# Modulation sums pinned to their traced place, decay vectors ahead of the first output projection, and low parts and other GpSimd work on VectorE between layers

## Chip, cores and metric

The kernel runs on one core of a Trainium2 chip. The metric is the device time of one execution in microseconds (us); the time before is 1883.51 us, the median of three runs (1880.94 to 1884.3).

## The reference, cut to what matters

Four layers run over 512 sample tokens and 128 prompt tokens of width 1024, with mixers in the order differential attention, retention, HGRN2, differential attention:

```python
for l in range(4):
    shift, scale, gate = split(silu(c) @ w_mod[l] + b_mod[l], 3)   # one set for samples, one for prompts
    h = rms_norm(x, g_pre[l]) * (1 + scale) + shift
    y = mixer[l % 3](h, w_in, w_out, ...)                          # ends in (o * silu(g)) @ w_out
    x = x + gate * rms_norm(y, g_post[l])
```

Retention also needs powers of a decay: `log_g = log1p(-exp(decay_param))`, sixteen numbers (two directions by eight heads), and from them the vectors that scale keys, queries and states.

## The kernel before, in words

All tokens stay on the chip as five tiles of 128 tokens (`NT`), four of samples and one of prompts. The products run on TensorE in three passes, since each operand is cut into a high part that ScalarE writes (`hi`) and a low part, the operand less its high part (`lo`, L116): `xh*wh + xh*wl + xl*wh`. Weights come by DMA as `raw`, are cut into `whi` (ScalarE, L178) and `wlo` (VectorE, L116), and at most four such pairs are live. The layer's input `h` is kept transposed as `hh` and `hl`.

**Order of the work.** The program is written with a scheduling layer. TensorE's instructions keep the order in which the program traces them. On every other engine the layer chooses the order ahead of time, by a model: where an engine is free it takes, of the instructions that are ready, the one traced first. So an instruction that is ready early can be put far ahead of its place in the trace. On the chip each engine then runs its queue strictly in that order. `tc.issue_after(ins)` makes what the block under it traces on `ins`'s engine stand behind `ins` in that queue.

**Modulation sums.** The vectors shift, scale and gate of a coming layer are summed while another layer runs. `w_mod` is loaded in pieces of four rows (`mraw`, two buffers, `mod_load` L324). `mod_next(rows)` (L351) adds `rows` to a debt, `mod_owed`, and as long as one row is owed and a piece is there it traces one row: two products of 128x256, on VectorE as `macc += raw * smod` (L371), or, for the first of a block's eight rows, on ScalarE (L369). In the attention layers every second row goes to ScalarE (L369) and is added on VectorE (L373). After eight rows a block is full; when row six of the next block is traced, `mod_turn` has TensorE transpose the full block (L339) and VectorE reduce it (L343). `weave` (L258) runs two generators into one another, the mixer's heads (main) and the projections for what comes next (fill); after each unit of fill it calls `mod_next(got * self.mod_pace)`, where `mod_pace` is four rows for each piece of the layer's list (`MOD_IN`: 24, 48, 0 and 8 pieces in the four layers) over `PACE` (155, 245, 195 by kind). `mod_finish` (L382), called when the fill reaches the tail of a layer, does all rows that are left and sets the debt to 0. The rest of that tail still calls `mod_next`.

**Between two layers** `out_layer` multiplies by `w_out`. Its last part runs, for each of the five tiles, 24 matmuls (`run`, the second half of the columns), then the norm: `square` on ScalarE, `norm` (VectorE L454 and L394, the power on GpSimd L401), `finish` (VectorE L553, times the gate), a copy of the first half from `yo` into `yg` on GpSimd (L614), `xt += yg * rs` on VectorE (L619), the DMA out (L620), `pre` (ScalarE L408, VectorE L394, GpSimd L401, ScalarE L410), which gives the next layer's normed tile `xh` (three buffers), and `turn` (L413): eight transposes on TensorE (L419), the modulation on VectorE (L421, L422), and `put_h`, the cut into `hh` (ScalarE L446) and `hl` (L116, on VectorE for tiles 0 and 4, on GpSimd for 1, 2 and 3). `step(tt)` are the 24 matmuls of the next layer's first projection for a tile. TensorE's order is run 0 to 3, turn 0, turn 1, run 4, turn 2, step 0, turn 3, step 1, turn 4, steps 2 to 4.

**Retention** (`ret` L875) begins with the decay vectors (L880 to L911: two DMAs, some twenty small instructions on VectorE and ScalarE, one of them the logarithm), then head 0's projections (`ret_proj`), and then, head by head, `weave(ret_mix(h), ret_proj(h + 1))`. `ret_proj` of a head gives 38.8 us of fill by its own count: 20 units of 1.3 for values and gates and 16 of 0.8 for queries and keys. It ends with the cut of the keys, `kh` on ScalarE (L922) and `kl` on VectorE (L116). `ret_mix` takes 3.5, 9 and 11 us of fill (`RW`) between its parts, the first right before it uses `kh` and `kl` (L929 to L931), and ends with `head_out` (VectorE L648). Each head also builds a table of decays: `tabt` on GpSimd (L958), then VectorE L959, ScalarE L960, VectorE L961.

Of the kernel before, what the change touches and what calls it, by code (L numbers as in the profile page):

```python
# [11 lines left out]
F32 = mybir.dt.float32  # L12
# [3 lines left out]
AF = mybir.ActivationFunctionType  # L16
ALU = mybir.AluOpType
# [4 lines left out]
P = 128  # L22
# [66 lines left out]
class Net:  # L89
# [260 lines left out]

    def mod_next(self, rows):  # L351

        nc = self.nc
        self.mod_owed += rows
        while self.mod_owed >= 1 and self.modr:
            self.mod_owed -= 1
            l, b, i, raw = self.modr[0]
            k = self.mod_row
            first = i == k == 0
            if first:  # L360
                self.macc = self.mp.tile([P, 2, 256], F32, tag="macc", bufs=2, name="macc")
            part = self.macc if first else None
            pool = self.mod_pool if k % 2 else None
            if pool is not None:
                part = pool.tile([P, 2, 256], F32, tag="mpart", bufs=2, name="mpart")
            for j in range(2):
                m, c = self.macc[:, j, :], self.smod[:, 4 * i + k, j:j + 1]
                if part is not None:
                    nc.scalar.activation(part[:, j, :], raw[:, k, :], AF.Copy, scale=c)  # L369
                else:  # L370
                    nc.vector.scalar_tensor_tensor(out=m, in0=raw[:, k, :], scalar=c, in1=m, op0=ALU.mult, op1=ALU.add)  # L371
            if pool is not None:
                nc.vector.tensor_tensor(out=self.macc, in0=self.macc, in1=part, op=ALU.add)  # L373
            if 4 * i + k == 5:
                self.mod_turn()
            self.mod_row = (k + 1) % 4
            if k == 3:
                self.modr.pop(0)
                if i == 1:
                    self.modp = (l, b, self.macc)  # L380
                self.mod_load()
# [30 lines left out]
    def turn(self, pool, l, tt, xh):  # L412

        nc = self.nc
        mt = self.mods[l]
        v = 0 if tt < 4 else 1
        pt = self.two([P, KT, P])
        for k in range(KT):
            nc.tensor.transpose(pt[:, k, :], xh[:, k * 128:k * 128 + 128], self.ident)  # L419
        h = pool.tile([P, KT, P], F32, tag="h32", bufs=2, name="h32")  # L420
        nc.vector.tensor_tensor(out=h, in0=pt, in1=mt[:, 8:16, v:v + 1].to_broadcast([P, KT, P]), op=ALU.mult)  # L421
        nc.vector.tensor_tensor(out=h, in0=h, in1=mt[:, 0:8, v:v + 1].to_broadcast([P, KT, P]), op=ALU.add)  # L422
        self.put_h(h, tt, nc.vector if tt in (0, 4) else None)

    def enter(self, l):

# [90 lines left out]
    def out_layer(self, l, y):  # L517
        nc, tc = self.nc, self.tc
        last = l == self.depth - 1
# [4 lines left out]
        with tc.tile_pool(name=f"op{l}", bufs=1, reuse_waits="tile") as op:  # L524
            w1 = self.take(l, 512, 4, op, nc.vector) if two else None
            xt = []
# [5 lines left out]
            yo = op.tile([P, NT, 2 if two else 1, 512], F32, name="yo")  # L532
            xh = {}
# [17 lines left out]
            def finish(tt, c, src, out):  # L551

                nc.vector.tensor_tensor(out=out, in0=src, in1=gb[:, 0 if tt < 4 else 1, c * 512:c * 512 + 512], op=ALU.mult)  # L553
# [53 lines left out]
            for tt in range(NT):  # L607
                ps = self.one()
                run(ps, tt, w1)
                if two:  # L610
                    nc.vector.tensor_tensor(out=yo[:, tt, 1, :], in0=yo[:, tt, 1, :], in1=ps, op=ALU.add)
                    ps = yo[:, tt, 1, :]
                yg = xh[tt] = op.tile([P, D], F32, tag="xh", bufs=3, name="xh")
                nc.gpsimd.tensor_copy(yg[:, 0:512], yo[:, tt, 0, :])  # L614
                square(tt, 1, ps)
                rs = self.norm(op, ssq[:, tt, :])
                finish(tt, 1, ps, yg[:, 512:1024])
                for c in (slice(0, 512), slice(512, 1024)) if last and tt == 4 else (slice(0, 1024),):
                    nc.vector.scalar_tensor_tensor(out=xt[tt][:, c], in0=yg[:, c], scalar=rs, in1=xt[tt][:, c], op0=ALU.mult, op1=ALU.add)  # L619
                    (nc.scalar if c.start else nc.sync).dma_start(self.x_out[tt][:, c], xt[tt][:, c])  # L620
                if not last:
                    self.pre(op, xt[tt], xh[tt])
                    for i in {3: (0, 1), 4: (2,)}.get(tt, ()):
                        self.turn(op, l + 1, i, xh[i])
            if not last:
                for tt in range(NT):
                    step(tt)
                    if tt < 2:
                        self.turn(op, l + 1, tt + 3, xh[tt + 3])


    def gate(self, o, ps):
# [239 lines left out]
        nc.vector.scalar_tensor_tensor(out=pr[1], in0=pr[1], scalar=rc, in1=pr[0], op0=ALU.mult, op1=ALU.add)  # L872


    def ret(self, l, y):  # L875
        nc, tc, t = self.nc, self.tc, self.t
        with tc.tile_pool(name=f"re{l}", bufs=1, reuse_waits="tile") as mp:
            self.gain = None
            rx = self.const(mp, "rx")
            rdec = self.const(mp, "rdec").rearrange("p (a b) -> p a b", a=2)  # L880
            rkd = self.const(mp, "rkd")
            e = mp.tile([P, 16], F32, name="dec_e")
            nc.sync.dma_start(e, t["ret_decay"][0].rearrange("a b -> (a b)").partition_broadcast(P))
            u = mp.tile([P, 16], F32, name="dec_u")
            d = mp.tile([P, 16], F32, name="dec_d")
            z = mp.tile([P, 16], F32, name="dec_z")
            lg = mp.tile([P, 2, 8], F32, name="lg")
            lgf = lg.rearrange("p a b -> p (a b)")
            ts_ = nc.vector.tensor_scalar
            nc.scalar.activation(e, e, AF.Exp)  # L890
            ts_(out=u, in0=e, scalar1=-1.0, scalar2=1.0, op0=ALU.mult, op1=ALU.add)
            ts_(out=d, in0=u, scalar1=1.0, scalar2=None, op0=ALU.subtract)
            ts_(out=z, in0=d, scalar1=0.0, scalar2=None, op0=ALU.is_equal)
            nc.vector.tensor_tensor(out=d, in0=d, in1=z, op=ALU.subtract)
            nc.vector.reciprocal(d, d)
            nc.vector.tensor_tensor(out=d, in0=d, in1=e, op=ALU.mult)
            nc.vector.tensor_tensor(out=z, in0=z, in1=e, op=ALU.mult)
            nc.scalar.activation(lgf, u, AF.Ln)
            nc.vector.tensor_tensor(out=lgf, in0=lgf, in1=d, op=ALU.mult)
            nc.vector.tensor_tensor(out=lgf, in0=lgf, in1=z, op=ALU.add)  # L900
            ts_(out=lgf, in0=lgf, scalar1=-1.0, scalar2=None, op0=ALU.mult)
            kd = mp.tile([P, 8, 6], F32, name="kd")
            for c0, c1, dr in ((0, 2, 0), (2, 4, 1), (4, 5, 0), (5, 6, 1)):
                n = c1 - c0
                nc.vector.tensor_tensor(out=kd[:, :, c0:c1], in0=rkd[:, c0:c1].unsqueeze(1).to_broadcast([P, 8, n]),
                                        in1=lg[:, dr, :].unsqueeze(2).to_broadcast([P, 8, n]), op=ALU.mult)
            nc.scalar.activation(kd, kd, AF.Exp)
            nlgb = mp.tile([P, 8], F32, name="nlgb")
            ts_(out=nlgb, in0=lg[:, 1, :], scalar1=-1.0, scalar2=None, op0=ALU.mult)
            cd = mp.tile([P, 2, 8], F32, name="cd")  # L910
            nc.scalar.activation(cd, lg, AF.Exp, scale=256.0)  # L911
            st = types.SimpleNamespace(mp=mp, l=l, lg=lg, kd=kd, cd=cd, rx=rx, rdec=rdec, nlgb=nlgb, h={})
            for _ in self.ret_proj(st, 0):
                pass
            for h in range(HEADS):
                fill = self.ret_proj(st, h + 1) if h < 7 else self.tail(l, y, 2, st)
                self.weave(self.ret_mix(st, h, y), fill, 1.0, 1.0 if h < 7 else RW[3])
# [15 lines left out]
    def ret_proj(self, st, h):  # L933
        nc, t, mp, lg = self.nc, self.t, st.mp, st.lg
# [20 lines left out]

        tab = hd.tab = mp.tile([P, 384], F32, tag="tab", bufs=2, name="tab")
        tb = mp.tile([P, 384], F32, tag="dq", name="tabt")
        nc.gpsimd.tensor_scalar(out=tb, in0=st.rx, scalar1=st.nlgb[:, h:h + 1], scalar2=None, op0=ALU.mult)  # L958
        nc.vector.scalar_tensor_tensor(out=tab, in0=st.rx, scalar=lg[:, 0, h:h + 1], in1=tb, op0=ALU.mult, op1=ALU.min)  # L959
        nc.scalar.activation(tab, tab, AF.Exp)  # L960
        nc.vector.scalar_tensor_tensor(out=tab, in0=st.rx, scalar=0.0, in1=tab, op0=ALU.is_equal, op1=ALU.add)  # L961
# [415 lines left out]
    def layers(self, depth):  # L1377
        nc, tc, t = self.nc, self.tc, self.t
# [13 lines left out]
        for l in range(depth):  # L1392
# [14 lines left out]
            with tc.tile_pool(name=f"y{l}", bufs=1, reuse_waits="tile") as yp_:  # L1407
                y = yp_.tile([P, NT, D], F32, name="y")
                (self.diff, self.ret, self.hg)[kind](l, y)
                self.out_layer(l, y)  # L1410
            self.x_in = self.x_out

# [31 lines left out]
```

## Time and profile before

| | |
|---|---|
| median of 3 runs | 1883.51 us |
| the profiled execution's own time | 1883.0 us |
| its span, first to last instruction | 1881.2 us |
| mean granted TensorE clock | 0.992 of full speed |
| TensorE matmul busy | 1803.2 us (96%) |
| VectorE, ScalarE, GpSimd busy | 1307.0 (69%), 981.3 (52%), 301.3 us (16%) |

PE is TensorE, PEld its weight loads, DVE VectorE, ACT ScalarE, POOL GpSimd, SP the queue that issues most DMAs. A matmul's shown time overlaps the next one's, so a busy PE is not a PE at its peak; an idle PE is lost time all the same, since its order is fixed and it is the busiest engine. Layer 0 runs to about 430 us, layer 1 to 1030, layer 2 to 1450, layer 3 to the end.

### The profile page before, as it was taken

Reading aid. Unit: us, or ns where it says so; the run is one execution under the profiler, and the core shown is the slowest. Engines: PE = TensorE matmul, PEld = TensorE weight load, DVE = VectorE, ACT = ScalarE, POOL = GpSimd, SP = SyncE. Lnnn points to the kernel's source line nnn. Section 1 sums busy time; section 2 is a strip of 40 time slices with the busy share of each in tenths; the row PEclk is TensorE's granted clock in tenths of the full one; section 3 lists DMA queues with packets and bytes.
Section 4 is the critical chain, followed back from the end, with each engine's and each line's share of the span. In section 5 each row is a group of like instructions: output and inputs, shape, how many; then the busy total and the mean of one; then the engine's idle time right before and its main releaser. Section 6 shows DMA issues by size and latency. Waiting matters only on the chain.

```text
span 1881.2 us, 31937 instructions
## 1 busy us (share of the span) xinstructions
PE 1803.2 (96%) x12060; PEld 1648.3 (88%) x12060; DVE 1307.0 (69%) x2681; ACT 981.3 (52%) x2271; POOL 301.3 (16%) x249
## 2 busy tenths in 40 slices
PE   6999999999999999999999999999979999999998
PEld 4889999977888888889878899999968889999976
DVE  4768888847788898873335666676774766767654
ACT  3556666645544444443333366666664645655552
POOL 0000000003222223222101223332331300000001
PEclk9999999999999999999999999999989999999999
DMA  9645455414354445443323322222214463443322
GB/s 302 181 122 151 146 146 166 122 51 157 117 160 146 149 150 158 124 135 101 115 93 101 96 71 66 63 63 74 62 43 135 140 171 91 116 114 100 100 73 101
DMA packets 231536, 224.39 MB, mean 119 GB/s; under 512 B 11619, under 2 KB 201558, under 8 KB 231382
## 3 DMA queue, kind: packets, MB, share of 16 engines
q1 hardware_dynamic: 230912, 221.96, 39.4%
q8 instruction: 95, 1.56, 0.4%
q14 instruction: 59, 0.48, 0.1%
q10 hardware_dynamic: 470, 0.39, 0.1%
HBM read 174.59 MB, written 18.35 MB: 103 GB/s over the span
## 4 chain that ended last, share of the span: by engine, by line
PE 62%; DVE 17%; ACT 8%; DMA 5%; issue 4%; POOL 2%; SPq 1%; DVEq 0%; ACTq 0%; POOLq 0%
PE one L474 6%; PE one L476 6%; PE one L475 6%; PE one L250 5%; PE one L251 5%; PE one L252 5%; DVE macc L371 3%; PE one L830 3%; PE one L225 3%; PE one L226 3%; PE one L227 3%; DVE wlo L116 2%; PE two L792 2%; PE two L793 2%; ACT whi L178 1%
## 5 line engine op out<-in xcount | busy, mean ns | idle before, releaser
L250 PE MATMUL one<-hh,whi 128*128 128x320 f32 x1152 | 364.6, 316 | 3.3 <-ACT qp L769 1.8
L252 PE MATMUL one<-hh,wlo 128*128 128x320 f32 x1152 | 356.1, 309 | 0.1
L251 PE MATMUL one<-hl,whi 128*128 128x320 f32 x1152 | 356.2, 309 | 0.0
L116 DVE TENSOR_TENSOR wlo<-raw,whi 128x1024 fp32r<-128x1024 f32 x192 | 235.8, 1234 | 142.6 <-ACT whi L178 142.1
L474 PE MATMUL one<-whi,hh 128*128 128x512 f32 x744 | 301.1, 405 | 6.5 <-ACT yo L569 3.2
L476 PE MATMUL one<-whi,hl 128*128 128x512 f32 x744 | 293.6, 395 | 1.7 <-DVE ms L394 1.3
L475 PE MATMUL one<-wlo,hh 128*128 128x512 f32 x744 | 292.2, 393 | 0.0
L178 ACT ACTIVATE whi<-raw 128x1024 fp32r<-128x1024 f32 x192 | 201.5, 1056 | 155.3 <-PE one L251 58.4
L250 PEld LDWEIGHTS one<-hh,whi 128*128 128x128 f32 x1152 | 216.9, 188 | 5.3 <-ACT qp L769 2.2
L251 PEld LDWEIGHTS one<-hl,whi 128*128 128x128 f32 x1152 | 217.1, 188 | 0.5
L252 PEld LDWEIGHTS one<-hh,wlo 128*128 128x128 f32 x1152 | 216.9, 188 | 0.4 <-DVE wlo L116 0.4
L401 POOL TENSOR_TENSOR rs<-ms,mhalf 128x1 f32<-128x1 f32 (+1 forms) x72 | 65.6, 913 | 901.3 <-DVE ms L399 724.8
L371 DVE SCALAR_TENSOR_TENSOR macc<-mraw,smod,macc 128x256 f32<-128x256 f32 x432 | 209.1, 527 | 0.2
L225 PE MATMUL one<-whi,hh 128*128 128x256 f32 x720 | 207.5, 288 | 0.0
L226 PE MATMUL one<-wlo,hh 128*128 128x256 f32 x720 | 200.8, 279 | 0.0
L227 PE MATMUL one<-whi,hl 128*128 128x256 f32 x720 | 200.8, 279 | 0.0
L474 PEld LDWEIGHTS one<-whi,hh 128*128 128x128 f32 x744 | 140.9, 189 | 36.9 <-DVE p L1017 4.0
L476 PEld LDWEIGHTS one<-whi,hl 128*128 128x128 f32 x744 | 140.5, 189 | 36.0 <-DVE hl L116 2.2
L475 PEld LDWEIGHTS one<-wlo,hh 128*128 128x128 f32 x744 | 140.9, 189 | 27.4
L225 PEld LDWEIGHTS one<-whi,hh 128*128 128x128 f32 x720 | 135.3, 188 | 1.5
L226 PEld LDWEIGHTS one<-wlo,hh 128*128 128x128 f32 x720 | 135.4, 188 | 0.0
L227 PEld LDWEIGHTS one<-whi,hl 128*128 128x128 f32 x720 | 135.0, 187 | 0.0
(345 smaller groups left out, 3548.6 us busy)
## 6 DMA issues: line engine op xcount, KB each, us to landing
mraw<-in_w_mod SPq DMA_DIRECT2D x96, 512.0 KB, 4.4
raw<-in_da_w_in SPq DMA_DIRECT2D x56, 512.0 KB, 4.5
raw<-in_hg_w_in SPq DMA_DIRECT2D x36, 512.0 KB, 3.9
raw<-in_ret_w_in SPq DMA_DIRECT2D x64, 256.0 KB, 3.1
kk<-ks SPq DMA_DIRECT2D x64, 160.0 KB, 2.8
kz<-ks SPq DMA_DIRECT2D x64, 160.0 KB, 2.8
qq<-q SPq DMA_DIRECT2D x64, 128.0 KB, 3.0
raw<-in_da_w_out SPq DMA_DIRECT2D x16, 512.0 KB, 3.4
```

The costliest lines, as they stand in the source:

```text
L116: return (eng or self.nc.gpsimd).tensor_tensor(out=out, in0=full, in1=hi.bitcast(F32), op=ALU.subtract)
L178: self.nc.scalar.activation(hi, raw, AF.Copy)
L225: mm(out, xh, wh[:, k % 4, :], start=(first and k == ks[0]), stop=False)
L226: mm(out, xh, wl[:, k % 4, :], start=False, stop=False)
L227: mm(out, xl, wh[:, k % 4, :], start=False, stop=(last and k == ks[-1]))
L250: nc.tensor.matmul(ps, wh[:, k, :], self.hh[:, k, c], start=(k == 0), stop=False)
L251: nc.tensor.matmul(ps, wh[:, k, :], self.hl[:, k, c], start=False, stop=False)
L252: nc.tensor.matmul(ps, wl[:, k, :], self.hh[:, k, c], start=False, stop=(k == KT - 1))
L371: nc.vector.scalar_tensor_tensor(out=m, in0=raw[:, k, :], scalar=c, in1=m, op0=ALU.mult, op1=ALU.add)
L474: mm(ps, xh, wh, start=(first and k == ks[0]), stop=False)
L475: mm(ps, xh, wl, start=False, stop=False)
L476: mm(ps, xl, wh, start=False, stop=(last and k == ks[-1]))
```

## The change

Four edits, all in the diff below. The modulation sums of a call of `mod_next` are put behind the VectorE and ScalarE instructions traced last before that call. The decay vectors move, unchanged, out of `ret` into a function `decay` that is traced after layer 0's mixer and before its output projection, in a pool that lives for the whole program. Between layers all low parts are made on VectorE, the GpSimd copy goes, the update of `xt` is two instructions of 512 columns and reads `yo` itself, and each turn of a tile comes one step later: run 0 to 3, turn 0, run 4, turn 1, step 0, turn 2, step 1, turn 3, step 2, turn 4, steps 3 and 4. `tabt` moves from GpSimd to VectorE.

```diff
     def mod_next(self, rows):
+        with ExitStack() as order:
+            for ins in self.traced():
+                order.enter_context(self.tc.issue_after(ins))
+            self.mod_rows(rows)
+
+    def traced(self):
+        found = {}
+        for ins in reversed(self.nc.cur_bb.bb.instructions):
+            if ins.engine in (mybir.EngineType.DVE, mybir.EngineType.Activation):
+                found.setdefault(ins.engine, ins)
+                if len(found) == 2:
+                    break
+        return list(found.values())
+
+    def mod_rows(self, rows):
         nc = self.nc
         self.mod_owed += rows
         while self.mod_owed >= 1 and self.modr:
...
-        self.put_h(h, tt, nc.vector if tt in (0, 4) else None)
+        self.put_h(h, tt, nc.vector)
...
                 yg = xh[tt] = op.tile([P, D], F32, tag="xh", bufs=3, name="xh")
-                nc.gpsimd.tensor_copy(yg[:, 0:512], yo[:, tt, 0, :])
                 square(tt, 1, ps)
                 rs = self.norm(op, ssq[:, tt, :])
                 finish(tt, 1, ps, yg[:, 512:1024])
-                for c in (slice(0, 512), slice(512, 1024)) if last and tt == 4 else (slice(0, 1024),):
-                    nc.vector.scalar_tensor_tensor(out=xt[tt][:, c], in0=yg[:, c], scalar=rs, in1=xt[tt][:, c], op0=ALU.mult, op1=ALU.add)
-                    (nc.scalar if c.start else nc.sync).dma_start(self.x_out[tt][:, c], xt[tt][:, c])
+                split = last and tt == 4
+                for c, half in ((slice(0, 512), yo[:, tt, 0, :]), (slice(512, 1024), yg[:, 512:1024])):
+                    nc.vector.scalar_tensor_tensor(out=xt[tt][:, c], in0=half, scalar=rs, in1=xt[tt][:, c], op0=ALU.mult, op1=ALU.add)
...
+                if not split:
+                    nc.sync.dma_start(self.x_out[tt], xt[tt])
                 if not last:
                     self.pre(op, xt[tt], xh[tt])
-                    for i in {3: (0, 1), 4: (2,)}.get(tt, ()):
-                        self.turn(op, l + 1, i, xh[i])
+                    if tt > 2:
+                        self.turn(op, l + 1, tt - 3, xh[tt - 3])
             if not last:
                 for tt in range(NT):
                     step(tt)
-                    if tt < 2:
-                        self.turn(op, l + 1, tt + 3, xh[tt + 3])
+                    if tt < 3:
+                        self.turn(op, l + 1, tt + 2, xh[tt + 2])
...
+    def decay(self):
+        nc, t, cp = self.nc, self.t, self.cp
...
+        self.decays = lg, kd, cd, nlgb
...
-        nc.gpsimd.tensor_scalar(out=tb, in0=st.rx, scalar1=st.nlgb[:, h:h + 1], scalar2=None, op0=ALU.mult)
+        nc.vector.tensor_scalar(out=tb, in0=st.rx, scalar1=st.nlgb[:, h:h + 1], scalar2=None, op0=ALU.mult)
...
                 (self.diff, self.ret, self.hg)[kind](l, y)
+                if l == 0:
+                    self.decay()
                 self.out_layer(l, y)
```

## Rows read from the trace of the kernel before

**Rows 1.** The page's first part: busy us, share of the span, instructions.
```profile
PE 1803.2 (96%) x12060; PEld 1648.3 (88%) x12060; DVE 1307.0 (69%) x2681; ACT 981.3 (52%) x2271; POOL 301.3 (16%) x249
```

**Rows 2.** Windows: stretch, length, busy us (instructions) of PE, PEld, DVE, ACT, POOL; PEclk.
```profile
65.00:112.00 47.00, 41.84 (x262) 39.59 (x260) 37.41 (x96) 25.58 (x67) 0.00 (x0) 0.96 0.73 210
115.00:350.00 235.00, 234.31 (x1830) 231.22 (x1828) 197.07 (x474) 157.60 (x443) 7.01 (x6) 1.00 0.48 138
440.00:480.00 40.00, 35.55 (x168) 28.86 (x167) 34.45 (x53) 19.13 (x31) 14.28 (x13) 0.96 0.38 122
505.00:520.00 15.00, 13.20 (x68) 10.50 (x67) 12.38 (x25) 7.21 (x16) 6.88 (x6) 1.00 0.31 89
520.00:840.00 320.00, 314.58 (x1849) 281.70 (x1848) 274.38 (x612) 136.21 (x308) 87.55 (x64) 1.00 0.48 148
1030.00:1056.00 26.00, 23.05 (x114) 18.95 (x113) 19.81 (x21) 10.87 (x16) 12.10 (x7) 1.00 0.21 72
```

**Rows 3.** Timeline between layers 0 and 1: start, us, instruction [idle before <-releaser].
```profile
463.79 3.03 DVE L371 SCALAR_TENSOR_TENSOR macc<-mraw,smod,macc 128x256 f32<-128x256 f32 x2
...
469.85 2.06 DVE L371 SCALAR_TENSOR_TENSOR macc<-mraw,smod,macc 128x256 f32<-128x256 f32 x5
...
471.58 1.09 PE L419 MATMUL two<-c_ident,xh 128*128 128x128 f32 x8 [3.50 <-ACT xh L410]
```

**Rows 4.** Groups by line: xcount | busy us, mean ns | idle before.
```profile
L619 DVE SCALAR_TENSOR_TENSOR xt<-xh,rs,xt 128x1024 f32<-128x1024 f32 (+1 forms) x21 | 27.9, 1334 | 11.0 <-POOL rs L401 11.0
L422 DVE TENSOR_TENSOR h<-h,modT 128x1024 f32<-128x1024 f32 x15 | 22.8, 1528 | 0.1
L116 POOL TENSOR_TENSOR hl<-h,hh 128x1024 fp32r<-128x1024 f32 x9 | 22.7, 2528 | 12.5 <-ACT hh L446 12.5
L421 DVE TENSOR_TENSOR h<-two,modT 128x1024 f32<-128x1024 f32 x15 | 18.0, 1217 | 7.4 <-PE two L419 7.4
L446 ACT ACTIVATE hh<-h 128x1024 fp32r<-128x1024 f32 x15 | 15.8, 1054 | 25.3 <-DVE h L422 25.2
L958 POOL TENSOR_SCALAR tabt<-c_rx,nlgb 128x384 f32<-128x384 f32 x8 | 13.2, 1652 | 14.7 <-DVE qd L978 8.1 <-DVE nlgb L909 6.5
```

**Rows 5.** Timeline between layers 1 and 2, the update of a tile.
```profile
1034.95 3.42 DVE L619 SCALAR_TENSOR_TENSOR xt<-xh,rs,xt 128x1024 f32<-128x1024 f32 x1 [0.43 <-POOL rs L401]
```

**Rows 6.** Waits of PE from 60 to 115 us: us, times, longest.
```profile
PE two L792 <- DMA raw<-in_da_w_in: 2.2, 1, 2.2
PE one L250 <- ACT qp L769: 1.3, 1, 1.3
```

**Rows 7.** Windows of L371 alone, 455 to 511 us: DVE busy (instructions).
```profile
455.00:511.00 56.00, 16.46 (x28) 0.97 0.37 116
```

**Rows 8.** Timeline at the start of layer 1.
```profile
485.68 1.28 ACT L898 ACT_TABLE_LOAD   x1
...
505.05 0.39 PE L474 MATMUL one<-whi,hh 128*128 128x512 f32 x1
...
506.44 0.60 PE L339 MATMUL one<-c_ident,macc 128*128 128x128 f32 x4
...
510.00 0.61 ACT L922 ACTIVATE kh<-k 128x512 fp32r<-128x512 f32 x1
...
511.26 0.68 DVE L116 TENSOR_TENSOR kl<-k,kh 128x512 fp32r<-128x512 f32 x1
```

**Rows 9.** Windows of DVE from a head's last L648 to the next kl.
```profile
556.10:568.00 11.90, 11.90 (x27) 1.00 0.62 194
667.40:678.30 10.90, 10.90 (x24) 1.00 0.52 159
```

**Rows 10.** The same windows, L371 alone.
```profile
556.10:568.00 11.90, 6.78 (x15) 1.00 0.62 194
667.40:678.30 10.90, 5.96 (x12) 1.00 0.52 159
```

**Rows 11.** Waits of PE from 520 to 840 us.
```profile
PE one L931 <- DVE kl L116: 1.8, 3, 0.6
```

More of the change, by code (lines that the diff above doesn't have):

```diff
@@ L617, in out_layer @@
                 finish(tt, 1, ps, yg[:, 512:1024])
-                for c in (slice(0, 512), slice(512, 1024)) if last and tt == 4 else (slice(0, 1024),):
-                    nc.vector.scalar_tensor_tensor(out=xt[tt][:, c], in0=yg[:, c], scalar=rs, in1=xt[tt][:, c], op0=ALU.mult, op1=ALU.add)
-                    (nc.scalar if c.start else nc.sync).dma_start(self.x_out[tt][:, c], xt[tt][:, c])
+                split = last and tt == 4
+                for c, half in ((slice(0, 512), yo[:, tt, 0, :]), (slice(512, 1024), yg[:, 512:1024])):
+                    nc.vector.scalar_tensor_tensor(out=xt[tt][:, c], in0=half, scalar=rs, in1=xt[tt][:, c], op0=ALU.mult, op1=ALU.add)
+                    if split:
+                        (nc.scalar if c.start else nc.sync).dma_start(self.x_out[tt][:, c], xt[tt][:, c])
+                if not split:
+                    nc.sync.dma_start(self.x_out[tt], xt[tt])
                 if not last:
                     self.pre(op, xt[tt], xh[tt])
-                    for i in {3: (0, 1), 4: (2,)}.get(tt, ()):
-                        self.turn(op, l + 1, i, xh[i])
+                    if tt > 2:
+                        self.turn(op, l + 1, tt - 3, xh[tt - 3])
             if not last:
@@ L872, in combine @@
         nc.vector.scalar_tensor_tensor(out=pr[1], in0=pr[1], scalar=rc, in1=pr[0], op0=ALU.mult, op1=ALU.add)
+    def decay(self):
+        nc, t, cp = self.nc, self.t, self.cp
+        rkd = self.const(cp, "rkd")
+        e = cp.tile([P, 16], F32, name="dec_e")
+        nc.sync.dma_start(e, t["ret_decay"][0].rearrange("a b -> (a b)").partition_broadcast(P))
+        u = cp.tile([P, 16], F32, name="dec_u")
+        d = cp.tile([P, 16], F32, name="dec_d")
+        z = cp.tile([P, 16], F32, name="dec_z")
+        lg = cp.tile([P, 2, 8], F32, name="lg")
+        lgf = lg.rearrange("p a b -> p (a b)")
+        ts_ = nc.vector.tensor_scalar
+        nc.scalar.activation(e, e, AF.Exp)
+        ts_(out=u, in0=e, scalar1=-1.0, scalar2=1.0, op0=ALU.mult, op1=ALU.add)
+        ts_(out=d, in0=u, scalar1=1.0, scalar2=None, op0=ALU.subtract)
+        ts_(out=z, in0=d, scalar1=0.0, scalar2=None, op0=ALU.is_equal)
+        nc.vector.tensor_tensor(out=d, in0=d, in1=z, op=ALU.subtract)
+        nc.vector.reciprocal(d, d)
+        nc.vector.tensor_tensor(out=d, in0=d, in1=e, op=ALU.mult)
+        nc.vector.tensor_tensor(out=z, in0=z, in1=e, op=ALU.mult)
+        nc.scalar.activation(lgf, u, AF.Ln)
+        nc.vector.tensor_tensor(out=lgf, in0=lgf, in1=d, op=ALU.mult)
+        nc.vector.tensor_tensor(out=lgf, in0=lgf, in1=z, op=ALU.add)
+        ts_(out=lgf, in0=lgf, scalar1=-1.0, scalar2=None, op0=ALU.mult)
+        kd = cp.tile([P, 8, 6], F32, name="kd")
+        for c0, c1, dr in ((0, 2, 0), (2, 4, 1), (4, 5, 0), (5, 6, 1)):
+            n = c1 - c0
+            nc.vector.tensor_tensor(out=kd[:, :, c0:c1], in0=rkd[:, c0:c1].unsqueeze(1).to_broadcast([P, 8, n]),
+                                    in1=lg[:, dr, :].unsqueeze(2).to_broadcast([P, 8, n]), op=ALU.mult)
+        nc.scalar.activation(kd, kd, AF.Exp)
+        nlgb = cp.tile([P, 8], F32, name="nlgb")
+        ts_(out=nlgb, in0=lg[:, 1, :], scalar1=-1.0, scalar2=None, op0=ALU.mult)
+        cd = cp.tile([P, 2, 8], F32, name="cd")
+        nc.scalar.activation(cd, lg, AF.Exp, scale=256.0)
+        self.decays = lg, kd, cd, nlgb
     def ret(self, l, y):
@@ L880, in ret @@
             rdec = self.const(mp, "rdec").rearrange("p (a b) -> p a b", a=2)
[L881 to L911, printed above, removed]
+            lg, kd, cd, nlgb = self.decays
             st = types.SimpleNamespace(mp=mp, l=l, lg=lg, kd=kd, cd=cd, rx=rx, rdec=rdec, nlgb=nlgb, h={})
```

## The prediction

> **What bounds the kernel now.** I began with the page's busy shares: TensorE is busy 96% of the span, VectorE 69%, ScalarE 52%, GpSimd 16% [rows 1]. TensorE's order is fixed by the trace of the program, so the change can only win back, or add, TensorE idle time and stretches at its low clock. The windows say where these lie near the change: in layer 0's start TensorE is busy 41.84 of 47 us, between layers 0 and 1 35.55 of 40, at layer 1's start 13.20 of 15, between layers 1 and 2 23.05 of 26; in the rest of layer 0 and in retention's first heads it is near full while VectorE is at 197.07/235 = 84% and 274.38/320 = 86% [rows 2]. That is the frame: some 15 us of idle time at four places, and two long stretches where VectorE has only 14 to 16% to spare.
>
> The timeline then says who causes the idle. Between layers 0 and 1 TensorE waits 3.50 us for an `xh` (L410) whose chain stands behind sums L371: two took 3.03 us beside a GpSimd low part, five 2.06 without one, 0.41 each [rows 3]. Though traced later, 28 sums ran between 455 and 511 us, 16.46 us of VectorE [rows 7]: the scheduler had moved layer 1's sums up into layer 0's tail. So far that when TensorE came to the first transposes of the sums (L339) at 506.44 us, before head 0's `kl` had even run (511.26) [rows 8], the block was finished.
>
> **The change, part by part** (against the profiled execution's own 1883.0 us, 1881.2 of it span; the median of the runs is 0.5 higher).
>
> *a. Start of layer 0.* Idle 47 − 41.84 = 5.2 us; the named waits are 1.3 for `qp` and 2.2 for weights [rows 6]. Sums pinned behind the rope's VectorE work no longer stand ahead of it, and their loads of `mraw` come later than the weights'. Bounds 0 and −5.2. I take −3, nearer the two waits (3.5) than the whole.
>
> *b. Rest of layer 0.* VectorE has 235 − 197.07 = 38 us free [rows 2], and takes the sums that (a) moves out, at 0.41 each [rows 3]. Nearly covered; bounds 0 and +4 (the weights' low parts could come late a few times). I take +1.
>
> *c. Between layers 0 and 1.* Idle 40 − 35.55 = 4.45, and a clock of 0.96 costs 40 × 0.04 = 1.6: 6.05 in all [rows 2]. A turn's path is now L421 1.2, L422 1.2 to 1.5, `hh` 1.05 [rows 4], and a low part of about 1.2 on VectorE in place of 2.53 on GpSimd [rows 4] (estimate: the L421 row, the same shape with two operands): some 4.7 us. TensorE runs 24 matmuls between a turn's transposes and their use; at 35.55/168 = 0.21 us [rows 2] that is 5.1, and the next turn's eight transposes add 1.09 [rows 3]. It fits, by 0.4 to 1.5 us. Splitting the update of `xt` adds less than the 0.41 us that a whole sum of 256 columns takes [rows 3], once a tile, inside the norm's own slack; the GpSimd copy vanishes off the path. Bounds 0 and −6.1; I take −5.6, since sums and GpSimd, both named by the wait, are gone.
>
> *d. Start of layer 1, the bill for (c).* `mod_finish` clears the debt when layer 0's tail begins, but the rest of that tail still calls `mod_next`: five units of 0.66, four of 3.9, one of 1.2 and four of 1.3 make 25.3 us of fill, times 96/155 = 0.62: 15.7 rows. No piece is loaded then, so all 16 rows are traced in one burst at layer 1's first unit of fill, right behind head 0's `kh` and `kl`. After eight of them comes the turn. Before, TensorE met it 506.44 − 505.05 = 1.4 us behind the last key projection X [rows 8]. Now it must wait for `kl` and seven rows of sums (the eighth is ScalarE's): 14 × 0.41 [rows 3] = 5.7 us. When is `kl` done? At the earliest X + 1.9: `kh` 0.61, `kl` 0.68 [rows 8] and about 0.6 to read the projection. At the latest X + 6.9 as before (511.26 + 0.68 − 505.05); but there the sums held it up. I take X + 2.9, near the early end. Stall: 2.9 + 5.7 − 1.4 = 7.2. After an idle stretch the clock fell in [rows 2] (0.96), costing 1.6; I add that, and take off the 15 − 13.20 = 1.8 idle that stands here now [rows 2]. Together +7.0. Bounds: +4 (early `kl`, no clock loss) and +11 (late `kl`).
>
> *e. Retention's heads with sums, five of them.* From a head's last L648 to the next head's `kl` VectorE is already without a gap: 11.90 of 11.90 and 10.90 of 10.90 us [rows 9], of which 15 and 12 sums are 6.78 and 5.96 [rows 10]. TensorE waits for that `kl` three times, 1.8 us together, at most 0.6 [rows 11]. `weave` spends 3.5 + 9 + 11 = 23.5 of a head's 38.8 us of fill between the parts of the head, so 15 are left behind its end: 15 × 4 × 48/245 = 12 rows, about 20 sums on VectorE. So about six more than now must pass before `kl`: 6 × 0.42 = 2.5 us. `tabt` on VectorE adds about 0.4 (1.65 on GpSimd [rows 4]; estimate from a 256-column sum at 0.41). Lower: the sums now run earlier in the head and slack takes it, less the GpSimd collisions removed, −2 in all. Upper: five heads × 2.4 = +12. I take +6, halfway: the full windows speak for the bill, and each wait's slack (at most 0.6 late now) is not seen.
>
> *f. Between layers 1 and 2.* Idle 26 − 23.05 = 2.95 [rows 2]. No sums run here; it is GpSimd: an `xt` update took 3.42 us [rows 5] against a mean of 1.33 [rows 4], beside a low part. All four low parts and the copy leave. Bounds 0 and −2.9; I take −2.7.
>
> *g. Decay vectors.* Some twenty small instructions, two DMAs on SP's queue and two loads of ScalarE's function table, 1.28 us each [rows 8], go to where layer 0 has a gap. ScalarE is at 157.60 of 235 there [rows 2], so I take +0.4; bounds 0 and 2 × 1.28 = +2.6. The Trainium skill, "ScalarE: Activation LUTs", section "What ACT_TABLE_LOAD costs", says a switch of set costs 1.28 us of load and then some 1.38 of drain, 2.66 in all; this case's row agrees on the load, and no row here shows the drain. By that page the upper bound would be 5.3, and the time in rival 4 below about 1891.
>
> Sum: −3 + 1 − 5.6 + 7.0 + 6 − 2.7 + 0.4 = **+3.1, so 1886.1 us**, some 1886.
>
> **Rivals.**
>
> *1. Faster.* VectorE's slack takes the heads (e between −2 and 0), and the burst is short (d at +4): −3 + 1 − 5.6 + 4 − 1 − 2.7 + 0.4 = −6.9, 1876. For it: a head still has 14% of VectorE free [rows 2]; against: none of it lies ahead of `kl` [rows 9].
>
> *2. Slower: sums ahead of `kl`.* One mechanism: pinned sums that VectorE cannot finish before TensorE needs `kl`, in every head in full (e +12) and at head 0 with the late `kl` (d +11). −3 + 1 − 5.6 + 11 + 12 − 2.7 + 0.4 = +13, 1896. It decides where more sums stand between a head's last L648 and `kl` than the 12 to 15 of now [rows 10], for with no gap there each further one costs 0.41 straight. For it: the waits for `kl` exist [rows 11]. Against: they are short.
>
> *3. The pin does not bind.* It puts sums behind the last traced instruction of the queue only; if that one is itself moved up, sums follow it. Then d and e fall away, the sums stay in (c), and only GpSimd's part goes: about half of (c) and all of (f), −3 − 2.7 = −6, 1877. Against: the last traced instruction is mostly one that waits for TensorE, and cannot move far.
>
> *4. Table loads on the path* (g +2.6): 1888. Against: ScalarE's free third of layer 0.
>
> **How the numbers follow.** The measurement tells about 0.2%, 3.8 us, from no change: 1879.7 to 1887.3 counts as the same. The forecast, 1881 to 1891, has 0.46 (0.28 within the band, 0.18 above, for e is open upward); rival 1, 1870 to 1880, 0.28 (0.26 faster, 0.02 the same); rival 2, 1891 to 1900, 0.16; rival 3 0.08 (0.07 faster, 0.01 the same); rival 4 0.02, slower. So faster 0.33, same 0.31, slower 0.36. The range 1874 to 1896 leaves out the outer parts of rivals 1 and 2, some 0.18; since cases of both signs hold most of the chance, the forecast's own 1881 to 1891 stands beside it.
>
> **What would show it.** Right: no L371 between layers 0 and 1, and L419 there without waits for `xh`; at layer 1's start one wait of TensorE at L339 for `macc`, about 7 us, with a dip of the clock behind it; in the heads longer waits of L931 for `kl`, 1 to 2 us each; no wait for `qp` at layer 0's start; no GpSimd low part between layers 1 and 2, and idle there near zero; the table loads before layer 0's end. Wrong: L339's wait missing or under 3 us (d falls, about 1880); waits for `kl` still under 0.6 (e falls, about 1880); sums still ahead of `kh` at layer 1's start (rival 3); TensorE waiting for `hl` or `xh` between layers (c and f fall, up to +8); new waits for `wlo` in layer 0's middle (b).

## The result and the profile after

The changed kernel takes 1908.93 us (median of 4 runs, 1907.49 to 1912.37) beside 1883.24 for the kernel before on the same chip: ratio 1.0139, 95% interval 1.0127 to 1.0151, 25.7 us slower. The forecast was 1886, within 1874 to 1896: wrong. The profiled execution took 1912.37 us, with a span of 1910.6, so the traces of the two differ by 29.4 us.

The page's first part, as in [rows 1]:

```profile
PE 1814.7 (95%) x12060; PEld 1652.0 (86%) x12060; DVE 1320.7 (69%) x2717; ACT 976.3 (51%) x2271; POOL 244.9 (13%) x212
```

No engine has much more to do: VectorE gains 14 us in all [rows 1], and GpSimd loses 56. Of the 29.4 us, 17.9 are time in which TensorE stands still (1910.6 − 1814.7 = 95.9 after, 1881.2 − 1803.2 = 78.0 before). The other 11.5 are TensorE's busy time, at a mean granted clock of 0.985 in place of 0.992. The clock is not the main thing: the fastest of the four runs had 0.992 too, and took 1907.49 us. The question is where the standing still lies. Line numbers moved: L371 is now L387, L369 L385, L419 L435, L619 L635, L823 L842, L931 L956.

TensorE issues 12060 matmuls in both kernels, in nearly the same order, so the start of the same matmul can be compared in two traces. The table gives, for the number of a matmul, how much later it starts than in the kernel before (minus is earlier); differences between columns are the price of a stage. Later experiments are in it too. Each row is one profiled execution, and these lie up to 5.2 us below (lag8) and 4.5 above (no_pin) the median of their kernel. For the heads (3300 to 5250), five kernels with the same pin in layer 1 show 14.1 to 17.3 us, so a difference of 3 us between two rows is no reading there.

```text
matmul number         500    590   2950   3150   3300   5250   6050   6300   9300   9900  12050
at, in before (us)    103    118    451    497    526    866   1025   1076   1467   1565   1872
after                -4.9   -1.4  +11.1   +4.5  +15.4  +29.6  +31.1  +28.9  +30.6  +30.9  +29.5
no_pin               -1.1   -1.1   -1.2   -3.7   -2.5   -0.6   +2.5   +0.3   -0.3   +5.0   +3.8
pin_only             -6.0   -2.8  +10.1   +3.4  +13.2  +27.9  +27.9  +28.4  +28.8  +27.7  +27.5
pin_after_layer0     -2.5   -2.3   -1.9   -8.4   +2.1  +19.4  +22.4  +20.2  +20.6  +20.4  +19.2
no_burst             -5.9   -2.7   +9.5   +2.9   +2.4  +28.2  +29.9  +27.7  +28.2  +27.9  +26.2
layer0_dve_only      -5.9   -3.2   +7.6   +1.2  +12.0  +27.5  +29.5  +27.3  +28.0  +27.0  +25.9
layer0_act_only      -5.9   -2.3   +5.9   -0.8  +11.3  +25.4  +28.4  +26.2  +25.8  +25.6  +24.6
lag8                 -5.9   +4.7   +9.5   +6.2   +5.9  +10.9  +11.0   +8.9   +6.8   +6.0   +4.8
floor                -2.0   -1.3   -1.6   -8.2   -6.5   -5.4   -5.3   -7.5   -5.4   -0.2   -1.3
mixed                -1.6   -1.0   -0.8   -6.4   -4.4   -3.1   -1.6   -3.9   -4.9   -6.1   -7.3
turn_late            -4.9   -1.6  +18.4  +13.0  +23.5  +38.4  +41.3  +39.2  +38.4  +38.1  +41.0
```

Row "after" gives the change by stage: the rest of layer 0 costs 12.5 us (−1.4 to +11.1), between layers 0 and 1 the change wins 6.6 (+11.1 to +4.5), the start of layer 1 costs 10.9, the heads with sums 14.2, and between layers 1 and 2 it wins 2.2. Three losses, two gains.

**Layer 0.** The two longest waits of TensorE from 115 to 350 us (us in total, times, longest); before, the list had one wait of 0.5 us:

```profile
PE one L849 <- ACT at L842: 7.4, 6, 2.3
PE one L839 <- ACT at L841: 2.3, 3, 0.9
```

The timeline at the longest of them, ScalarE and TensorE:

```profile
338.96 0.89 ACT L385 ACTIVATE macc<-mraw,smod 128x256 f32<-128x256 f32 x2
339.76 0.89 ACT L385 ACTIVATE mpart<-mraw,smod 128x256 f32<-128x256 f32 x2
340.56 0.58 ACT L841 ACTIVATE at<-one 128x512 f32<-128x512 f32 x1
341.04 0.27 ACT L842 ACTIVATE at<-one 128x128 f32<-128x128 f32 x1
...
341.35 0.38 PE L849 MATMUL one<-v,at 128*128 128x128 f32 x1 [2.29 <-ACT at L842]
```

Four products of sums stand right ahead of `at`, the copy that TensorE needs next: 1.6 us of sums (338.96 to 340.56) inside a wait of 2.29. VectorE's adds wait in turn, each for the product it takes in (DVE's waits in the same stretch):

```profile
DVE macc L389 <- ACT mpart L385: 11.0, 4, 4.0
```

**Between the layers.** The windows that answer to [rows 2] (the columns are those of [rows 2]), at their new places: between layers 0 and 1, start of layer 1, heads, between layers 1 and 2:

```profile
455.00:482.00 27.00, 26.48 (x132) 21.65 (x131) 19.56 (x27) 12.01 (x17) 3.75 (x6) 1.00 0.34 116
511.00:530.00 19.00, 8.65 (x38) 7.22 (x38) 16.19 (x38) 5.27 (x12) 0.59 (x1) 0.64 0.37 111
541.00:896.00 355.00, 342.99 (x1953) 302.03 (x1952) 282.78 (x627) 143.12 (x324) 76.27 (x61) 0.99 0.44 135
1061.00:1084.00 23.00, 22.94 (x111) 18.55 (x110) 17.30 (x22) 9.35 (x12) 3.58 (x4) 1.00 0.23 81
```

The idle of 4.45 us between layers 0 and 1 is down to 0.52 of 27, the 2.95 between layers 1 and 2 to 0.06 of 23, both at full clock. The window of L387 alone from 460 to 516 us shows no sum at all, where [rows 7] has 28:

```profile
460.00:516.00 56.00, 0.00 (x0) 0.98 0.28 95
```

**Start of layer 1.** What was taken away there comes due here: TensorE is busy 8.65 of 19 us, at 0.64 of its full clock. VectorE's timeline, and TensorE's behind it:

```profile
510.82 1.18 DVE L984 SCALAR_TENSOR_TENSOR tab<-c_rx,lg,tabt 128x384 f32<-128x384 f32 x1
512.59 0.56 DVE L986 SCALAR_TENSOR_TENSOR tab<-c_rx,tab 128x384 f32<-128x384 f32 x1 [0.59 <-ACT tab L985]
514.34 1.23 DVE L116 TENSOR_TENSOR wlo<-raw,whi 128x1024 fp32r<-128x1024 f32 x1 [1.19 <-ACT whi L178]
515.48 0.69 DVE L116 TENSOR_TENSOR kl<-k,kh 128x512 fp32r<-128x512 f32 x1
516.08 5.63 DVE L387 SCALAR_TENSOR_TENSOR macc<-mraw,smod,macc 128x256 f32<-128x256 f32 x14
...
509.54 0.39 PE L490 MATMUL one<-whi,hh 128*128 128x512 f32 x1
...
510.71 0.40 PE L492 MATMUL one<-whi,hl 128*128 128x512 f32 x1
521.46 1.21 PE L339 MATMUL one<-c_ident,macc 128*128 128x128 f32 x4 [10.35 <-DVE macc L387]
```

Right behind `kl` come 14 sums in 5.63 us, and TensorE waits 10.35 us for them at L339: about half of that for what stands ahead of the sums, half for the sums.

**Heads.** TensorE's longest waits from 541 to 896 us answer to [rows 11]:

```profile
PE one L339 <- DVE macc L387: 5.0, 5, 1.7
PE one L250 <- DVE sg L655: 2.8, 2, 1.4
PE one L956 <- DVE kl L116: 1.4, 1, 1.4
PE one L1045 <- DVE p L1042: 1.3, 1, 1.3
```

The wait for `kl`, 1.8 us in [rows 11], has not grown. The waits at L339 for the sums themselves are new, and the two at L250 took 1.6 us before. In the same matmuls before, TensorE was idle for 5.4 us, and after for 12.0 (third line of the four windows above):

```profile
525.59:866.37 340.78, 335.36 (x1953) 299.20 (x1951) 278.35 (x618) 144.11 (x323) 92.54 (x67) 1.00 0.46 140
```

That is 6.6 of the 14.2 us. The other 7.6 are busy time; two falls of the clock (last section) explain about half of it, and the rest has no name in the profile.

The length of a head is read from one `kl` to the next. One head before (from the second to the third `kl` after head 0's), then the same head after: all engines, then the sums alone.

```profile
622.70:678.40 55.70, 54.21 (x319) 48.38 (x317) 50.71 (x115) 24.58 (x55) 14.27 (x11) 1.00 0.49 153
622.70:678.40 55.70, 27.34 (x54) 1.00 0.49 153
```

```profile
640.80:699.10 58.30, 56.27 (x326) 49.51 (x324) 48.76 (x114) 24.02 (x56) 13.28 (x10) 1.00 0.46 144
640.80:699.10 58.30, 25.88 (x53) 1.00 0.46 144
```

VectorE does the same work, 54 and 53 sums among it, and is busy 50.71 of 55.70 us before and 48.76 of 58.30 after. The head is 2.6 us longer though VectorE is less full. It is order, not volume; the runs without the pin, below, bear this out.

### The profile page after: what moved, and what is told of

Same layout as the page of the kernel before. It is cut to its first block, busy times and chain, and to the rows that moved or that the text cites. A ratio compares the mean times of both kernels' runs of the same rounds, so it can differ in the third digit from the quotient of the medians.

```text
span 1910.6 us, 31838 instructions
## 1 busy us (share of the span) xinstructions
PE 1814.7 (95%) x12060; PEld 1652.0 (86%) x12060; DVE 1320.7 (69%) x2717; ACT 976.3 (51%) x2271; POOL 244.9 (13%) x212
## 4 chain that ended last, share of the span: by engine, by line
PE 61%; DVE 15%; ACT 10%; DMA 7%; issue 3%; SPq 3%; POOL 1%; ACTq 0%; DVEq 0%; POOLq 0%
PE one L492 7%; PE one L490 7%; PE one L491 7%; PE one L250 5%; PE one L251 5%; PE one L252 5%; PE one L849 3%; PE one L225 3%; PE one L226 3%; PE one L227 3%; DVE macc L387 2%; DVE wlo L116 2%; DMA mraw<-in_w_mod 2%; SPq L763 2%; ACT whi L178 2%
## 5 line engine op out<-in xcount | busy, mean ns | idle before, releaser
L250 PE MATMUL one<-hh,whi 128*128 128x320 f32 x1152 | 363.7, 316 | 2.8 <-DVE sg L655 2.8
L250 PEld LDWEIGHTS one<-hh,whi 128*128 128x128 f32 x1152 | 217.2, 189 | 4.2 <-issue 3.2
L387 DVE SCALAR_TENSOR_TENSOR macc<-mraw,smod,macc 128x256 f32<-128x256 f32 x432 | 207.9, 527 | 8.0 <-DMA mraw<-in_w_mod 6.0
```

The source lines that it names most:

```text
L250: nc.tensor.matmul(ps, wh[:, k, :], self.hh[:, k, c], start=(k == 0), stop=False)
```

## The experiments

The theory: the pin causes all of the loss, in three separate places, and the rest of the change is neutral or a small gain. The rival: the work moved to VectorE (the table of decays, the low parts) costs part of it.

### The change without the pin

```diff
     def mod_next(self, rows):
-        with ExitStack() as order:
-            for ins in self.traced():
-                order.enter_context(self.tc.issue_after(ins))
-            self.mod_rows(rows)
+        self.mod_rows(rows)
```

> The change without its pin: sums may be moved up again, the other three edits stand. Theory (the pin causes all of the loss): layer 0's middle, layer 1's start and the heads come back to the times of before (-12, -12 and -13 us against the changed kernel), idle between layers 1 and 2 stays gone (-2.5 against before), and part of the idle between layers 0 and 1 returns because the sums are there again: 1877 to 1881 us. Rival (the table of decays and the low parts on VectorE carry part of the loss in the heads): 1886 us or more, with waits of TensorE in retention's heads longer than before's.

Measured: 1882.23 us beside 1884.1, ratio 0.9991 (0.9980 to 1.0002): the time of before. The table's row no_pin shows none of the three losses; of the two gains, 2.5 us between layers 0 and 1 (−1.2 to −3.7), where sums run again, and 2.2 between layers 1 and 2 remain. It loses 5.3 us at the start of layer 3 (matmul 9300 to 9900), and it comes out above the theory's 1877 to 1881. The rival falls: the heads with sums come out 1.9 us above before in all (−2.5 to −0.6), of a loss of 14.2.

### The pin alone on the kernel before

```diff
+    def mod_next(self, rows):
+        with ExitStack() as order:
+            for ins in self.traced():
+                order.enter_context(self.tc.issue_after(ins))
+            self.mod_rows(rows)
+
...
-    def mod_next(self, rows):
+    def mod_rows(self, rows):
```

> The kernel before with the pin alone. Theory: all of the loss (+36 us in layer 0's middle, layer 1's start and the heads) and some 4 us of gain between layers 0 and 1, where GpSimd's low parts stay; between layers 1 and 2 as before: 1911 to 1916 us. Rival (part of the loss is the table of decays on VectorE and the vectors' move): 1895 to 1905 us.

Measured: 1914.88 us, ratio 1.0175 (1.0152 to 1.0199), as the theory said, and the three losses stand at the same places (12.9, 9.8 and 14.7 us). Between layers 0 and 1 the pin alone wins 6.7 us, between layers 1 and 2 nothing. So the pin alone brings the whole first gain (the rest of the change, without it, 2.5), and the second belongs to the work taken off GpSimd.

### The pin from layer 1 on

```diff
+            self.pin = l > 0
...
-            for ins in self.traced():
+            for ins in self.traced() if self.pin else ():
```

> The change with the pin only from layer 1 on. Theory (in layer 0 the pinned products on ScalarE and adds on VectorE wait for one another and hold up the attention's copies): layer 0 is 11 us shorter, the rest as in the changed kernel: 1897 to 1899 us, no waits of TensorE for the copy `at` (L842, 7.4 us) between 115 and 350 us. Rival (the sums that are not done in layer 0's start must be done somewhere in layer 0, and cost the same wherever they stand): 1905 us or more.

Measured: 1902.99 us, ratio 1.0103 (1.0087 to 1.0119). Layer 0 is fully mended: −1.9 in place of +11.1 at 451 us, and between 115 and 350 us TensorE waits for one thing, shortly:

```profile
PE one L839 <- DVE pe L891: 0.6, 1, 0.6
```

The total is 4 us above the theory's range all the same, because the heads took more in this execution, 17.3 us in place of 14.2, though layer 1 is pinned just as in the changed kernel: that is scatter. The rival's claim, that the sums cost the same wherever they stand in layer 0, falls.

### One of the two queues pinned in layer 0

```diff
+            self.pin = l > 0
...
             for ins in self.traced():
-                order.enter_context(self.tc.issue_after(ins))
+                if self.pin or ins.engine == mybir.EngineType.DVE:
+                    order.enter_context(self.tc.issue_after(ins))
```

The second kernel has `Activation` in place of `DVE`.

> The change with only VectorE's instructions pinned while layer 0 runs (ScalarE's products free), both from layer 1 on. Theory (the 13 us of layer 0 need both pins: an add in its place on VectorE waits for a product that stands late on ScalarE, up to 4.0 us, and holds up what is behind it): layer 0 ends 2 to 6 us later than with no pin there: 1903 to 1908 us less the heads' scatter. Rival (VectorE's pin alone does it): layer 0 12 us or more later, as in the changed kernel.

> The change with only ScalarE's products pinned while layer 0 runs (VectorE's sums and adds free), both from layer 1 on. Theory (both are needed): layer 0 ends 2 to 6 us later than with no pin there. Rival (ScalarE's pinned products alone stand in front of the copies `at` that TensorE waits for): 10 us or more later, and the waits for L842 are back.

Measured: 1911.66 us (ratio 1.0151, 1.0133 to 1.0170) and 1911.83 (1.0150, 1.0124 to 1.0175), which the medians cannot tell from the full change. The table is finer: with no pin in layer 0 matmul 2950 is at −1.9, with VectorE's alone at +7.6, with ScalarE's alone at +5.9, with both at +11.1. Either costs 8 to 10 us, both together 13. So the theory that it takes both falls; so does each rival that one does all, though with ScalarE's alone the waits for `at` are back as that rival said. TensorE's waits from 115 to 350 us with ScalarE pinned alone (lines one higher than in the changed kernel):

```profile
PE one L850 <- ACT at L843: 6.6, 6, 2.6
```

and with VectorE pinned alone (the longest two):

```profile
PE one L850 <- ACT at L843: 3.6, 4, 1.1
PE one L840 <- ACT qp L789: 2.6, 1, 2.6
```

ScalarE's pinned products stand ahead of `at` directly. With VectorE pinned alone ScalarE is late too, for its products now wait for VectorE's pinned adds, 13.5 us in this stretch (3.2 with no pin in layer 0), and what is behind them in its queue waits along:

```profile
ACT mpart L386 <- DVE macc L390: 13.5, 15, 1.9
```

### No burst at the start of layer 1

```diff
+            self.mod_owed = 0
             self.mod_pace, self.mod_pool = ...
```

> The change with the debt cleared when a layer begins, so that the 16 rows of the burst are spread over the layer by the pace instead. Theory (the wait of 10.4 us at L339 is the burst's): the wait at the first L339 of layer 1 falls to under 2 us with the clock dip behind it gone, 1897 to 1900 us. Rival (rows left out of the burst are paid for later, at other turns or at the end of the layer, where the rest of the rows are finished): 1903 us or more.

Measured: 1906.26 us, ratio 1.0122 (1.0107 to 1.0137). The burst's wait is gone: the start of layer 1 costs −0.5 (+2.9 to +2.4) in place of 10.9. And the rival is right about the rest: the heads cost 25.8 us in place of 14.2, and more sums stand in them (319 of L387 from 529 to 894 us, 296 after). TensorE's longest waits in the heads, 529 to 894 us:

```profile
PE one L956 <- DVE kl L116: 5.1, 4, 2.1
PE one L1045 <- DVE modT L343: 3.7, 2, 1.8
PE one L339 <- DVE macc L387: 3.5, 4, 1.2
```

With a pinned order the rows cost about the same at once or spread (25.1 us for start and heads together after, 25.3 here), so the burst was not just one bad place.

### The transposes of a block two rows later

```diff
-            if 4 * i + k == 5:
+            if 4 * i + k == 7:
                 self.mod_turn()
```

> The change with the transposes of a full block (L339) traced two rows later, right behind row eight of the next block in place of row six. Theory (in the heads TensorE mostly waits at L339 for the last pinned sums of a block, 5.0 us and two dips of the clock): those waits shrink, heads of 57 us in place of 58.5, the burst's wait as before: 1901 to 1905 us. Rival (the order on VectorE holds up the head's own work, and TensorE waits for that instead): heads of 58 us or more, waits for `kl`, `p` and `sg` longer, 1906 us or more.

Measured: 1921.38 us, ratio 1.0184 (1.0165 to 1.0203), the slowest of all. In the heads the wait at L339 nearly goes, and `kl` takes its place (TensorE's longest waits, 560 to 900 us):

```profile
PE one L956 <- DVE kl L116: 5.0, 4, 2.2
PE one L490 <- DVE p L1042: 2.3, 2, 1.3
PE one L250 <- DVE sg L655: 2.3, 2, 1.4
PE one L1045 <- DVE p L1042: 1.8, 1, 1.8
PE one L339 <- DVE macc L387: 0.8, 1, 0.8
```

The rival holds: whichever of VectorE's results is asked for first is late. The 12 us more come mostly from layer 0, which this edit moves too: matmul 2950 is 7.3 us later than in the changed kernel, TensorE now waiting at L339 between 115 and 350 us (5.3 us for VectorE's `sg`, 2.2 for ScalarE's `hsq`). Layer 3 behind its start adds 4.4 (matmul 9900 to 12050).

### Pins that leave some freedom

Two kernels let a sum move up, but not without bound. In the first it may stand up to eight calls ahead of its place:

```diff
+        self.back = (self.back + [self.traced()])[-9:]
         with ExitStack() as order:
-            for ins in self.traced():
+            for ins in self.back[0]:
```

> The change with each call's sums pinned not behind the newest VectorE and ScalarE instructions but behind those that were newest eight calls earlier, some 8 to 10 us of fill. Theory (the heads lose because a sum may not use the holes just ahead of its place): heads of 55 to 56.5 us in place of 58.5, layer 0's middle near the time of before: 1885 to 1894 us. Rival (sums must be moved up far, by a head or more, to help): heads of 58 us again, 1902 us or more.

In the second a layer's sums are kept behind the layer's start and nothing else, and the debt is cleared:

```diff
+            self.mod_owed, self.floor = 0, self.traced() if l else []
...
-            for ins in self.traced():
+            for ins in self.floor:
```

> The change with the sums of a layer kept behind the start of that layer only (no other pin), and the debt cleared when a layer begins. Theory (moving up within a layer is what the heads need, moving up across the start of layer 1 is what hurts): layer 0 as without the pin, between layers 0 and 1 as in the changed kernel (no sums, no wait for `xh`), a wait at the first L339 of layer 1 under 2 us, heads of 55 to 56 us each: 1874 to 1879 us, the fastest of all. Rival (the 30 sums that ran between the layers are missing later, and the heads take them on at their full price): heads of 57 us or more, 1884 us or more.

Measured: eight calls of freedom give 1892.85 us, ratio 1.0044 (1.0024 to 1.0063), with the heads' loss down from 14.2 us to 5.0 (+5.9 to +10.9), in an execution 5.2 us below the median. The rest of layer 0 costs 4.9 (+4.7 to +9.5) in place of 12.5; but 10.6 us are lost earlier, between 103 and 118 us, where TensorE waits 9.0 us for the attention's `pe` and `at`. The total is the theory's case, at its upper end. The floor gives 1883.63, ratio 1.0006 (0.9995 to 1.0018). The same head as above, all engines and the sums alone:

```profile
615.20:670.40 55.20, 54.76 (x321) 48.67 (x320) 50.88 (x112) 24.07 (x55) 13.32 (x10) 1.00 0.51 155
615.20:670.40 55.20, 27.86 (x56) 1.00 0.51 155
```

56 sums in a head of 55.20 us: that a sum may move up inside its layer is worth nearly all of the heads' loss (−6.5 to −5.4 is 1.1 left), and keeping it out of the stretch between the layers wins 6.6 us (−1.6 to −8.2) with only 1.7 given back behind it. The total misses the theory's 1874 to 1879 by what is lost at the start of layer 3: −5.4 to −0.2 from matmul 9300 to 9900, as in the kernel without the pin.

### Each stage in its best order

```diff
+            self.mod_owed, self.layer = 0, l
+            self.floor = self.traced() if l else []
...
-            for ins in self.traced():
+            for ins in self.traced() if self.layer == 3 else self.floor:
```

> The change with each place given the order that its run was best in: no pin in layer 0, sums of layer 1 kept behind the layer's start (debt cleared), the pin as in the changed kernel in layer 3. Theory (the free sums of layer 3 stand ahead of its rope and cost the 5 to 6 us seen there): 1877 to 1880 us, faster than both. Rival (layer 3's 6 us are scatter of its start, or the pinned sums cost as much later in the layer, as in layer 0): 1882 to 1886 us.

Measured: 1875.68 us (1872.41 to 1877.05) beside 1885.02, ratio 0.9948 (0.9935 to 0.9961): 0.5% faster than before and, by the two ratios (0.9948/1.0139), 1.9% faster than the changed kernel, a little under the range that the theory gave. With layer 3 pinned its start loses nothing (−4.9 to −6.1), as in every kernel pinned there, so the rival falls. The theory's reason, free sums ahead of the rope, is not shown: the kernel before, unpinned, has the same 12 sums and 24 products in that stretch as floor and no_pin, and takes 98.0 us for it, where they take 103. That the pin costs nothing here goes with a low pace, 32 rows over the whole layer; in layer 0 it is three times that.

## Why the prediction was wrong, step by step

- **b, rest of layer 0: the step that failed most.** Predicted +1, bounds 0 to +4; measured +12.5. "Nearly covered" rested on a share: 38 us free of VectorE in 235. A pinned sum cannot use free time that lies ahead of the place to which the pin ties it; with eight calls of freedom this stretch costs 4.9. And ScalarE's products, half the rows in the attention layers, were given no cost at all; alone they cost 8 us.
- **e, heads: the wrong deadline.** Predicted +6, upper bound +12; measured +14.2. The step put the whole bill on `kl`, about six more sums ahead of it in every head and waits of 1 to 2 us. There were between one and two more: between a head's last L667 (L648 before) and the next `kl` stand 16, 16, 10, 16 and 18 sums, where 15, 14, 12, 13 and 14 stood. The first and the third head, which answer to [rows 10]:

```profile
570.00:583.30 13.30, 6.95 (x16) 1.00 0.57 169
685.60:699.10 13.50, 4.25 (x10) 1.00 0.56 168
```

TensorE waited for `kl` once, 1.4 us, less than the 1.8 before. It waited instead at L339 for the pinned sums themselves (5.0 us, none before), and longer at L250 (2.8 for `sg`, 1.6 before), and the clock fell behind two of the waits. The step took one deadline for the bill where every result of VectorE is one. In no_burst and turn_late `kl` did become the longest wait, 5.1 and 5.0 us.
- **d, the burst: the mechanism was right, the size at its upper bound.** Predicted +7.0 (up to +11), measured +10.9. The 14 sums took 5.63 us (5.7 predicted). The term that was mis-sized is `kl`. The prediction's X, the start of the first 512-column matmul behind the key projection (505.05 in [rows 8]), lies at 509.54 us here; TensorE reached L339 at 511.11, 1.6 behind it (1.4 predicted), but `kl` ended at 516.17, 6.6 behind it in place of 2.9. The prediction took 2.9 because sums were said to have held up the 6.9 of before. That reading was wrong: VectorE's timeline of before shows no sum from 500 us to `kl` at 511.26, only the work that stood ahead of `kl` again, the decay table and a weight's low part above all. ScalarE's `kh`, at 514.60, was late behind the same table and the same weight.
- **c and f, between the layers: right.** −5.6 predicted, −6.6 measured, half a us beyond the bound; −2.7 and −2.2. No sum was left in the stretch, no wait for `xh` in either. For (c) the prediction named sums and GpSimd; pin_only wins all of it with GpSimd's work still there.
- **a, start of layer 0:** −3 predicted, −1.4 measured. The gain reached 4.9 at 103 us, the waits for weights and `qp` were gone, and 3.5 of it was given back within 15 us, where TensorE waited 3.4 for the attention's `pe` instead and the clock fell (a mean of 0.91 from 98 to 116 us). What is left is not the pin's for certain: without it (no_pin) this stage is 1.1 shorter too.
- **g, decay vectors: right, nothing seen.** Both table loads moved to the start of the program, where ScalarE has idle time; TensorE's longest wait from 25 to 60 us is 1.9, for a result of VectorE, as before (1.8):

```profile
35.89 1.28 ACT L914 ACT_TABLE_LOAD   x1
37.19 0.22 ACT L914 ACTIVATE lg<-dec_u 128x16 f32<-128x16 f32 x1
...
41.65 1.28 ACT L927 ACT_TABLE_LOAD   x1
42.94 0.22 ACT L927 ACTIVATE cd<-lg 128x16 f32<-128x16 f32 x1
```

The next ScalarE instruction starts 1.30 and 1.29 us behind a load. The drain of 1.38 us that the Trainium skill, "ScalarE: Activation LUTs", section "What ACT_TABLE_LOAD costs", adds to a load does not show here; the rows decide, and a switch cost 1.3.

With the terms as measured (−1.4 + 12.5 − 6.6 + 10.9 + 14.2 − 2.2, and 2.1 us scattered over the rest) the sum is +29.5, as the traces differ. Rival 2, pinned sums that VectorE cannot finish in time, came nearest to the mechanism; it was priced at 1896 because it had only `kl` for a deadline, which was not the one missed in the heads, and nothing in layer 0. Rival 3, a pin that does not bind, is excluded by the empty window of L387; rival 4 by the table loads' place.

## What to carry to other kernels

That an engine is 15% free in the mean does not say that work with a fixed place in its queue is free: holes ahead of that place are lost to it, and results behind it can come later. Here this cost in layers 0 and 1, and nothing in layer 3, where a third as many rows as in layer 0 were pinned. Work with a distant due time should have a window, a bound that keeps it from moving too far up, not an exact place. When a pin is priced, count each engine that it ties and each result asked for behind it, not only the one that was late before.

## What was not expected of the hardware

That short waits can double in price. At the wait of 10.35 us at the start of layer 1 TensorE's clock fell to the lower of its two levels (1.2 GHz), and behind the one of 3.50 us in [rows 3] it had done so before; but in the heads it fell behind waits below 2 us too, at 749 and 811 us. It did not behind every such wait: four others of 1.3 to 1.4 us, for `sg`, `p` and `kl`, were followed by none. Timeline of TensorE in a head of the changed kernel, and the two windows around the fall (columns as in [rows 2]):

```profile
808.97 0.85 PE L339 MATMUL one<-c_ident,macc 128*128 128x128 f32 x4 [1.74 <-DVE macc L387]
```

```profile
802.00:810.50 8.50, 6.75 (x46) 6.33 (x45) 8.50 (x20) 3.73 (x9) 2.85 (x3) 1.00 0.22 64
810.50:814.00 3.50, 3.50 (x13) 3.12 (x12) 3.07 (x7) 1.97 (x5) 0.44 (x1) 0.52 0.62 197
```

At 0.52 of the full clock, the second window's 3.50 us lose 3.50 × 0.48 = 1.7 us, as much as the wait itself. The prediction had charged such a fall for the burst alone.
